# Transposing attention probabilities on VectorE and through DRAM instead of on TensorE, in a one-core hybrid block

## The chip, the cores and the metric

One core of a Trainium2 chip runs the whole kernel. The metric is the device time of one execution in microseconds, taken as the median of repeated runs. TensorE (PE) multiplies matrices, VectorE (DVE) and ScalarE (ACT) work element by element, GpSimd (POOL) does some adds here and issues DMAs of its own, and SyncE (SP) issues the other DMAs. A queue of an engine is worked off in the order of the program: what stands behind a waiting instruction waits too.

## The reference

A decoder block on 256 tokens of width 2048, in fp32. What matters for the change is the attention; the rest is one stream of weight matmuls.

```
proj = rmsnorm(x) @ w_in                     # pooled branch, queries, keys, values, gate inputs
y_a  = (pool_mixer(u) * silu(g_pool)) @ w_pool_out
# per kv head (4), per query head of it (4): compressed, selected and window branch
p_c  = softmax(mask(q @ kc.T * scale))       # 15 compressed keys
p_s  = softmax(mask(qh @ ks.T * scale))      # selected keys (256 tokens: all 4 blocks)
p_w  = softmax(mask(qh @ kw.T * scale))      # window keys
o    = g0 * (p_c @ vc) + g1 * (p_s @ vs) + g2 * (p_w @ vw)
y_b  = (o * silu(g_nsa)) @ w_nsa_out
gm   = sigmoid(h @ w_merge + b_merge)
out  = rmsnorm(x + (gm0 * y_a + gm1 * y_b) @ w_out)
```

The probabilities come out of the softmax with the query tokens on the partitions. The products with the values need the keys there, so every block of probabilities is transposed.

## The kernel before

**Numbers.** Each fp32 operand is split into a high and a low float32r part (`split`, L209 ff.: ACT copies the high part at L214, DVE subtracts it for the low part at L215), and each product is three matmuls (`mm3`, L226 to L229): high by high, high by low, low by high.

**Order.** The weights are streamed from DRAM in 314 units of up to 512 KB, in the order of `plan()`. For i = 0 to 3 come the chunks q(i), gn(i), m(i) and po(i) with 8, 8, 8 and 4 units; later m, no and wo. A unit is 12 matmuls of 128x512. The loop of `body` issues the load of a unit on SP six units ahead (`AHEAD`), its split three units ahead (`CUT`), then the unit's matmuls, and then `advance()`, which takes one piece of work from each of the lanes "e", "a", "c", "d", "b" in turn. The lanes hold generators; a `yield` ends a piece. So the program's order of small work between the units is set by how often a generator yields.

**Queries.** When chunk q(i) is done, `evac_q` applies the rotary embedding: two multiplications on DVE (L495, L498) and an add on GpSimd (L499), for each of two token blocks. `queries(i)` in lane "a" then calls `turn()`: DVE transposes 32x32 blocks (L275, a tile q1R for head 1), GpSimd writes it to DRAM (L281, q1W) and reads it back with four DMAs that put the blocks in their places (L285, qT). After `TURN` = 4 pieces the result is split into qh and ql (L214, L215), and the two attention pairs of head i are put into lane "b". `gate_t` does the same for the gate (gn).

**Attention.** `attend(hk, pr)` handles pair pr (0 or 1) of kv head hk, two query heads g each. Scores are three products of 272, 272 and 256 columns per g; each goes to a buffer of the PSUM tag "S", of which there are two, and DVE adds the mask and frees it (L710). The names S1000, S1001 and S1002 in this document are the scores of head 1, pair 0, g 0, product 0, 1 and 2. Then come the maxima (L716 to L721), the exponentials on ACT (L731), and `weigh` (L742 to L750), which scales by gate and sum and leaves three weighted copies of the compressed part in Cn. The transposes are matmuls with the identity: four per g in `turn1` (L756, second token block), two per g in `turn0` (L763), and two of Cn (L798), into PSUM tag "T". Each group is split from PSUM by ACT and DVE into P1h, P1l, P0 and Pc. `values` multiplies with the values (L818 and `mm3`) some steps later.

The tiles of tag "B" (46 blocks of 128x1056) hold weights, their parts, queries, scores and probabilities alike.

Of the kernel before, what the change touches and what calls it, by code (L numbers as in the profile page):

```python
# [11 lines left out]
F32 = mybir.dt.float32  # L12
F32R = mybir.dt.float32r
BF16 = mybir.dt.bfloat16
AF = mybir.ActivationFunctionType
OP = mybir.AluOpType
# [172 lines left out]
def body(nc, tc, d, out):  # L189
# [5 lines left out]
    dp = tc.alloc_tile_pool(name="dp", bufs=1, space=bass.MemoryType.DRAM)  # L195

    def blk(dt, name):
        return sb.tile([128, NB], dt, tag="B", bufs=NBLK, name=name)
# [7 lines left out]
    def psum(tag, name):  # L206
        return pp.tile([128, 512], F32, tag=tag, bufs={"P": 4, "S": 2, "T": 2}[tag], name=name)

    mm, act, dve, pool = nc.tensor.matmul, nc.scalar.activation, nc.vector, nc.gpsimd  # L209

    def split(hi, lo, src, scale=None, eng=None):

        if scale is None:
            act(hi, src, AF.Copy)  # L214
            (eng or dve).tensor_tensor(lo, src, hi.bitcast(F32), op=OP.subtract)  # L215
        else:
            act(hi, src, AF.Copy, scale=scale)
            dve.scalar_tensor_tensor(lo, src, scale, hi.bitcast(F32), op0=OP.mult, op1=OP.subtract)
# [16 lines left out]
    def C(name):  # L235
        a, b = CONST[name]
        return ct[:, a:b]
# [5 lines left out]
    ss2 = cp.tile([128, 2, 5], F32, name="ss2")  # L243


    lanes = {k: deque() for k in "eacdb"}

    def later(lane, gen):
        lanes[lane].append(gen)
# [437 lines left out]
    def attend(hk, pr):  # L687
        nm = f"{hk}{pr}"
        Cn = small(192, f"Cn{nm}", bufs=2)
        Cv = Cn.rearrange("p (i c g n) -> p i c g n", i=2, c=3, g=2)  # L690
        P1h, P1l, P0 = blk(F32R, f"P1h{nm}"), blk(F32R, f"P1l{nm}"), blk(F32R, f"P0{nm}")
        v1h, v1l = (x[:, :1024].rearrange("p (k g q) -> p k g q", k=4, g=2) for x in (P1h, P1l))
        v0h, v0l = (P0[:, a:a + 512].rearrange("p (k g q) -> p k g q", k=2, g=2) for a in (0, 512))
        qh, ql = qTt[hk]
        Ss, cfs = {}, {}

        SC = ((0, 0, 272, 0, C("m0")), (1, 0, 272, 272, C("m1")), (1, 272, 528, 544, C("m0")[:, 16:]))

        def scores(g, js):
            hd = pr * 2 + g  # L700
            if g not in Ss:
                Ss[g] = blk(F32, f"S{nm}{g}")
            Sg = Ss[g]
            for j in js:
                tok, a, b, o, m = SC[j]
                ps = psum("S", f"S{nm}{g}{j}")[:, :b - a]
                qo = hd * 256 + tok * 128
                kh, kl = kth(hk, a, b)
                mm3(ps, qh[:, qo:qo + 128], ql[:, qo:qo + 128], kh, kl, True, True)
                dve.tensor_tensor(Sg[:, o:o + b - a], ps, m, op=OP.add)  # L710

        def probs(g):
            Sg = Ss[g]
            mx = small(6, f"mx{nm}{g}")
            sm = small(6, f"sm{nm}{g}")
            dve.tensor_reduce(mx[:, 1:3], Sg[:, 16:272].rearrange("p (b k) -> p b k", b=2), axis=AX.X, op=OP.max)  # L716
            t1 = Sg[:, 288:800].rearrange("p (k b c) -> p b k c", k=2, b=2)
            dve.tensor_reduce(mx[:, 4:6], t1, axis=AX.XY, op=OP.max)
            cc = Sg[:, :544].rearrange("p (i c) -> p i c", i=2)[:, :, :16]
            dve.tensor_reduce(mx.rearrange("p (i b) -> p i b", i=2)[:, :, 0], cc, axis=AX.X, op=OP.max)  # L720
            dve.tensor_scalar(mx, mx, -1e29, -SCALE, op0=OP.max, op1=OP.mult)  # L721
            cfs[g] = mx, sm

        def expo(g):
            Sg = Ss[g]
            mx, sm = cfs[g]
            for i in range(2):
                for b in range(3):
                    k = i * 3 + b
                    s = part(Sg, i, b)  # L730
                    act(s, s, AF.Exp, bias=mx[:, k:k + 1], scale=SCALE, accum_out=sm[:, k:k + 1])  # L731

        def part(Sg, i, b):
            if b == 0:
                return Sg[:, i * 272:i * 272 + 16]
            if i == 0:
                return Sg[:, b * 128 - 112:b * 128 + 16]
            return Sg[:, 288:800].rearrange("p (k b c) -> p b k c", k=2, b=2)[:, b - 1]

        def weigh(g):  # L740
            Sg, sm = Ss[g], cfs[g][1]
            dve.tensor_tensor(sm[:, 0:1], sm[:, 0:1], C("inval"), op=OP.add)  # L742
            dve.reciprocal(sm, sm)
            dve.tensor_tensor(sm, sm, gates[:, hk * 4 + pr * 2 + g].rearrange("p i b -> p (i b)"), op=OP.mult)
            for i in range(2):
                dve.tensor_scalar(Cv[:, i, :, g], part(Sg, i, 0)[:, None, :].to_broadcast([128, 3, 16]),
                                  sm[:, i * 3:i * 3 + 1], None, op0=OP.mult)
                for b in range(1, 3):
                    s = part(Sg, i, b)
                    dve.tensor_scalar(s, s, sm[:, i * 3 + b:i * 3 + b + 1], None, op0=OP.mult)  # L750

        def turn1(g):
            Sg = Ss[g]
            p1 = psum("T", f"p1{nm}{g}")
            for k in range(4):
                nc.tensor.transpose(p1[:, k * 128:k * 128 + 128], Sg[:, 288 + k * 128:416 + k * 128], C("ident"))  # L756
            split(v1h[:, :, g], v1l[:, :, g], p1.rearrange("p (k q) -> p k q", k=4))

        def turn0(g):
            Sg = Ss[g]  # L760
            p0 = psum("T", f"p0{nm}{g}")
            for k in range(2):
                nc.tensor.transpose(p0[:, k * 128:k * 128 + 128], Sg[:, 16 + k * 128:144 + k * 128], C("ident"))  # L763
            split(v0h[:, :, g], v0l[:, :, g], p0[:, :256].rearrange("p (k q) -> p k q", k=2))

        if pr == 0:
            yield
            yield
        scores(0, (0, 1))
        yield  # L770
        scores(0, (2,))
        probs(0)
        yield
        expo(0)
        yield
        scores(1, (0, 1))
        yield
        scores(1, (2,))
        probs(1)
        yield  # L780
        weigh(0)
        expo(1)
        yield
        yield
        turn1(0)
        yield
        turn0(0)
        weigh(1)
        yield
        yield  # L790
        turn1(1)
        yield
        turn0(1)
        yield

        pc = psum("T", f"pc{nm}")
        for i in range(2):
            nc.tensor.transpose(pc[:96, i * 128:i * 128 + 128], Cn[:, i * 96:i * 96 + 96], C("ident"))  # L798
        Pc = half(F32R, f"Pc{nm}")
        Pv = Pc[:96].rearrange("p (i g q) -> p i g q", i=2, g=2)  # L800
        pcv = pc[:96, :256].rearrange("p (i q) -> p i q", i=2)
        for g in range(2):
            act(Pv[:, :, g], pcv, AF.Copy, scale=C("pair")[:96, g:g + 1])
            dve.scalar_tensor_tensor(Pv[64:96, :, g], pcv[64:96], C("pair")[64:96, g:g + 1],
                                     Pv[64:96, :, g].bitcast(F32), op0=OP.mult, op1=OP.subtract)
        later("d", values(hk, pr, Pv, v0h, v0l, v1h, v1l))

    def values(hk, pr, Pv, v0h, v0l, v1h, v1l):
        nm = f"{hk}{pr}"
        yield  # L810
        yield
        po = psum("T", f"po{nm}")
        pov = po.rearrange("p (g t) -> p g t", g=2)
        hs = slice(hk * 128, hk * 128 + 128)
        hs2 = slice(512 + hk * 128, 640 + hk * 128)
        for i in range(2):
            o = pov[:, :, i * 128:i * 128 + 128]
            mm(o, vstk[:, hk], Pv[:, i], start=True, stop=False)  # L818
            n = 2 * (i + 1)
            vh, vl = (v0h, v0l) if i == 0 else (v1h, v1l)  # L820
            for k in range(n):
                V = Vt[k // 2, k % 2]
                mm3(o, V[:, hs], V[:, hs2], vh[:, k], vl[:, k], False, k == n - 1)
        yield
        if pr == 0:
            yTt[hk] = (blk(F32R, f"yh{hk}"), blk(F32R, f"yl{hk}"))
        t = half(F32, f"y{nm}")
        cs = slice(pr * 512, pr * 512 + 512)
        dve.tensor_tensor(t.rearrange("p (g c j) -> p g c j", g=2, j=32), po.rearrange("p (g c j) -> p g c j", g=2, j=32),
                          by_head(gnT[hk])[:, pr * 2:pr * 2 + 2], op=OP.mult)  # L830
        yield
        split(yTt[hk][0][:, cs], yTt[hk][1][:, cs], t, eng=pool)
# [306 lines left out]
TURN = 4  # L1139
NTURN = 4  # L1140
# [43 lines left out]
```

## Time and profile before

| | us |
|---|---|
| median of 3 runs | 900.69 (899.91 to 901.51) |
| the profiled execution | 899.8 |
| its span | 898.0 |
| PE busy | 888.4 (99%) |
| DVE busy | 593.7 (66%) |
| ACT busy | 464.0 (52%) |
| POOL busy | 156.7 (17%) |
| mean granted TensorE clock | 0.997 |

The span is the time from the first to the last instruction on the core; 1.8 us of the execution lie outside it. Busy shares are means over stages of different kinds. A chain of waits follows the work that ended last back from the end: its pieces don't overlap, while the durations of neighbouring matmuls do. A timeline gives start and duration of each instruction, and in brackets how long the engine was idle before it and what ended that. The name in brackets is the releaser that the profile infers; for a read-back behind its own write it can name another engine that happened to finish then.

### The profile page before, as it was taken

The page shows a single profiled execution, that of the slowest core. Times are in us where ns is not written, and L with a number is a line of the kernel's source. Part 1 is how long each engine was busy: PE and PEld are TensorE (multiplying, and loading weights), DVE is VectorE, ACT ScalarE, POOL GpSimd, SP SyncE. Part 2 cuts the span into 40 slices and gives each one's busy share as a digit, 9 for nine tenths or more (in the row PEclk, how much of TensorE's full clock was granted, in tenths as well). Part 3 has the DMA queues.
Part 4 walks back from the last instruction along what each step waited for, and adds up shares of the span by engine and source line. Part 5 has one row for each costly group of instructions (what it writes and reads, how often), then busy time and mean ns, then how long its engine had stood idle before and what let it go on. Part 6 is the DMA issues. An engine that isn't in the chain of part 4 may idle for free.

```text
span 898.0 us, 11882 instructions
## 1 busy us (share of the span) xinstructions
PE 888.4 (99%) x4289; PEld 748.0 (83%) x4289; DVE 593.7 (66%) x889; ACT 464.0 (52%) x726; POOL 156.7 (17%) x145
## 2 busy tenths in 40 slices
PE   9999999999999999999999999999999999999996
PEld 7999988888888888888888888888888888888886
DVE  7756457877747476868685868687765565547633
ACT  7666545635734365456645664566554434436510
POOL 2203235333002110212021202110002312111110
PEclk9999999999999999999999999999999999999998
DMA  9955675778865664576557654766566776986602
GB/s 341 401 171 181 220 257 182 230 240 286 282 232 177 194 202 147 170 218 201 172 155 215 210 167 139 241 203 213 171 194 218 233 223 214 305 292 213 218 1 93
DMA packets 56298, 189.02 MB, mean 210 GB/s; under 512 B 6960, under 2 KB 7728, under 8 KB 56240
## 3 DMA queue, kind: packets, MB, share of 16 engines
q1 hardware_dynamic: 50912, 172.40, 59.0%
q0 software_dynamic: 5040, 15.73, 5.8%
q8 instruction: 33, 0.54, 0.2%
q14 instruction: 25, 0.20, 0.1%
q10 hardware_dynamic: 288, 0.14, 0.1%
HBM read 178.29 MB, written 9.96 MB: 210 GB/s over the span
## 4 chain that ended last, share of the span: by engine, by line
PE 98%; DMA 1%; DVE 0%; ACT 0%; SPq 0%; issue 0%; DVEq 0%; ACTq 0%
PE m L229 7%; PE m L228 7%; PE m L227 7%; PE p L228 3%; PE p L227 3%; PE p L229 3%; PE wo L229 3%; PE gn L229 3%; PE gn L228 3%; PE q L228 3%; PE q L229 3%; PE wo L227 3%; PE no L228 3%; PE wo L228 3%; PE gn L227 3%; PE no L227 3%
## 5 line engine op out<-in xcount | busy, mean ns | idle before, releaser
L215 DVE TENSOR_TENSOR l<-w,h 128x1024 fp32r<-128x1024 f32 (+2 forms) x312 | 388.1, 1270 | 76.7 <-ACT h L214 69.3
L214 ACT ACTIVATE h<-w 128x1024 fp32r<-128x1024 f32 (+2 forms) x312 | 308.5, 1031 | 66.4 <-PE no L228 13.4
L227 PE MATMUL m<-h,xh 128*128 128x512 f32 x256 | 101.3, 396 | 0.0
L229 PE MATMUL m<-h,xl 128*128 128x512 f32 x256 | 100.9, 394 | 0.0
L228 PE MATMUL m<-l,xh 128*128 128x512 f32 x256 | 100.7, 393 | 0.0
L227 PE MATMUL p<-h,xh 128*128 128x420 f32 (+1 forms) x160 | 57.4, 359 | 0.4 <-ACT h L1090 0.3
L229 PEld LDWEIGHTS m<-h,xl 128*128 128x128 f32 x256 | 48.0, 188 | 11.2
L228 PE MATMUL p<-l,xh 128*128 128x420 f32 (+1 forms) x160 | 56.7, 354 | 0.2 <-DVE l L1096 0.2
L229 PE MATMUL p<-h,xl 128*128 128x420 f32 (+1 forms) x160 | 56.5, 353 | 0.0
L227 PEld LDWEIGHTS m<-h,xh 128*128 128x128 f32 x256 | 48.2, 188 | 9.9
L228 PEld LDWEIGHTS m<-l,xh 128*128 128x128 f32 x256 | 48.2, 188 | 10.0
L731 ACT ACTIVATE S<-S,mx 128x16 f32<-128x16 f32 (+2 forms) x96 | 37.7, 394 | 34.9 <-DVE mx L721 34.8
L227 PE MATMUL wo<-h,mh 128*128 128x512 f32 (+1 forms) x144 | 53.2, 369 | 0.0
L229 PE MATMUL wo<-h,ml 128*128 128x512 f32 (+1 forms) x144 | 53.1, 368 | 0.0
L228 PE MATMUL wo<-l,mh 128*128 128x512 f32 (+1 forms) x144 | 52.9, 367 | 0.0
L227 PE MATMUL gn<-h,xh 128*128 128x512 f32 x128 | 51.6, 403 | 0.0
L227 PE MATMUL q<-h,xh 128*128 128x512 f32 x128 | 51.0, 398 | 0.0
L229 PE MATMUL gn<-h,xl 128*128 128x512 f32 x128 | 50.4, 394 | 0.0
L229 PE MATMUL q<-h,xl 128*128 128x512 f32 x128 | 50.4, 394 | 0.0
L228 PE MATMUL gn<-l,xh 128*128 128x512 f32 x128 | 50.4, 394 | 0.0
L228 PE MATMUL q<-l,xh 128*128 128x512 f32 x128 | 50.4, 394 | 0.0
L228 PE MATMUL no<-l,yh 128*128 128x512 f32 x128 | 50.3, 393 | 0.0
(339 smaller groups left out, 1771.8 us busy)
## 6 DMA issues: line engine op xcount, KB each, us to landing
w<-wts SPq DMA_DIRECT2D x274, 512.0 KB, 4.2
w<-wts SPq DMA_DIRECT2D x30, 420.0 KB, 7.6
w<-wts SPq DMA_DIRECT2D x8, 416.0 KB, 3.7
bb<-bmr SPq DMA_DIRECT2D x8, 256.0 KB, 4.4
xr<-xn SPq DMA_DIRECT2D x4, 512.0 KB, 4.8
out<-ot SPq DMA_DIRECT2D x8, 256.0 KB, 2.5
xs<-xT SPq DMA_DIRECT2D x7, 256.0 KB, 7.3
bt<-bic SPq DMA_DIRECT2D x2, 512.0 KB, 8.5
```

The lines of the kernel that those rows point to most:

```text
L214: act(hi, src, AF.Copy)
L215: (eng or dve).tensor_tensor(lo, src, hi.bitcast(F32), op=OP.subtract)
L227: mm(o, ah, bh, start=start, stop=False)
L228: mm(o, ah, bl, start=False, stop=False)
L229: mm(o, al, bh, start=False, stop=stop)
L731: act(s, s, AF.Exp, bias=mx[:, k:k + 1], scale=SCALE, accum_out=sm[:, k:k + 1])
```

## The change

The 112 transposes on TensorE go. `turn_p(g)` puts in their place three block transposes on DVE per g (128x256 each; for g = 1 a fourth, of Cn, 128x192) into a tile R, one write to DRAM by GpSimd (tile Wp), and four reads back by GpSimd into a tile G (for g = 1 seven). `cut_p`, in a new lane "w" that stands ahead of "b", waits six pieces and then splits the parts of G into P1h, P1l and P0, one per piece, and Pc with the last. `attend` yields less: the second `weigh` comes one piece earlier, and the generator ends four pieces earlier, so that the next pair starts earlier. The layout of Pc and the view of the product with the compressed values follow.

```diff
-    lanes = {k: deque() for k in "eacdb"}
+    lanes = {k: deque() for k in "eacdwb"}
...
-        def turn1(g):
+        G = {}
+
+        def turn_p(g):
+
             Sg = Ss[g]
-            p1 = psum("T", f"p1{nm}{g}")
-            for k in range(4):
-                nc.tensor.transpose(p1[:, k * 128:k * 128 + 128], Sg[:, 288 + k * 128:416 + k * 128], C("ident"))
-            split(v1h[:, :, g], v1l[:, :, g], p1.rearrange("p (k q) -> p k q", k=4))
-
-        def turn0(g):
-            Sg = Ss[g]
-            p0 = psum("T", f"p0{nm}{g}")
-            for k in range(2):
-                nc.tensor.transpose(p0[:, k * 128:k * 128 + 128], Sg[:, 16 + k * 128:144 + k * 128], C("ident"))
-            split(v0h[:, :, g], v0l[:, :, g], p0[:, :256].rearrange("p (k q) -> p k q", k=2))
+            r = blk(F32, f"R{nm}{g}")
+            rv = r[:, :768].rearrange("p (b k j) -> p k b j", b=4, j=32)
+            for k, o in ((0, 16), (2, 288), (4, 544)):
+                dve.transpose(rv[:, k:k + 2], Sg[:, o:o + 256].rearrange("p (k b j) -> p k b j", k=2, b=4))
+            n = 768
+            if g:
+
+                dve.transpose(r[:, 768:960].rearrange("p (c i j) -> p i c j", c=3, j=32),
+                              Cn.rearrange("p (i c j) -> p i c j", i=2, j=32))
+                n = 960
+            w = dp.tile([128, 960], F32, tag="Wp", bufs=NTURN, name=f"Wp{nm}{g}")
+            pool.dma_start(w[:, :n], r[:, :n])
+            t = G[g] = blk(F32, f"G{nm}{g}")
+            for b in range(4):
+                pool.dma_start(t[32 * b:32 * b + 32, :768].rearrange("p (a x) -> p a x", a=4),
+                               w[:, b * 192:b * 192 + 192].rearrange("(a i) x -> i a x", a=4))
+            if g:
+                for c in range(3):
+                    pool.dma_start(t[32 * c:32 * c + 32, 768:1024].rearrange("p (a x) -> p a x", a=4),
+                                   w[:, 768 + c * 64:832 + c * 64].rearrange("(a i) x -> i a x", a=4))
...
         weigh(0)
         expo(1)
         yield
-        yield
-        turn1(0)
-        yield
-        turn0(0)
+        turn_p(0)
+        yield
         weigh(1)
         yield
-        yield
-        turn1(1)
-        yield
-        turn0(1)
-        yield
-
-        pc = psum("T", f"pc{nm}")
-        for i in range(2):
-            nc.tensor.transpose(pc[:96, i * 128:i * 128 + 128], Cn[:, i * 96:i * 96 + 96], C("ident"))
+        turn_p(1)
+        later("w", cut_p(hk, pr, G))
+
+    def cut_p(hk, pr, G):
+
+        nm = f"{hk}{pr}"
+        for _ in range(TURN + 2):
+            yield
+        P1h, P1l, P0 = blk(F32R, f"P1h{nm}"), blk(F32R, f"P1l{nm}"), blk(F32R, f"P0{nm}")
...
+        for g in range(2):
+            t = G[g][:, :768].rearrange("p (a k j) -> p k a j", a=4, j=32)
+            q4 = [x[:, :, g].rearrange("p k (a j) -> p k a j", j=32) for x in (v1h, v1l, v0h, v0l)]
+            split(q4[0], q4[1], t[:, 2:])
+            yield
+            split(q4[2], q4[3], t[:, :2])
+            if g == 0:
+                yield
         Pc = half(F32R, f"Pc{nm}")
-        Pv = Pc[:96].rearrange("p (i g q) -> p i g q", i=2, g=2)
-        pcv = pc[:96, :256].rearrange("p (i q) -> p i q", i=2)
+        Pv = Pc[:96].rearrange("p (g a i j) -> p i g a j", g=2, a=4, i=2)
+        pcv = G[1][:96, 768:1024]
```

In the rows of order below, a name's number tells buffers of one name apart; w, h and l are a weight unit and its two parts, yph and ypl the parts of the pooled branch.

TensorE at the first removed group, between the last unit of chunk m(0) and the first of po(0). Before:

```order
L227 MATMUL m_2850<-h_2965,xh_287 128x512
L228 MATMUL m_2850<-l_2966,xh_287 128x512
L229 MATMUL m_2850<-h_2965,xl_288 128x512
L756 MATMUL p_3063<-ct,S_2860 128x128 x4
L227 MATMUL po_3076<-h_2994,yph_1271 128x512
L228 MATMUL po_3076<-l_2995,yph_1271 128x512
```

Now:

```order
L227 MATMUL m_2847<-h_2962,xh_287 128x512
L228 MATMUL m_2847<-l_2963,xh_287 128x512
L229 MATMUL m_2847<-h_2962,xl_288 128x512
L227 MATMUL po_3086<-h_2991,yph_1271 128x512
L228 MATMUL po_3086<-l_2992,yph_1271 128x512
```

The four transposes of the scores' tile S are gone, and the units follow one another.

GpSimd ahead of the queries of head 2 (yl are low parts of the gated output). Before:

```order
L285 DMA gnT_3719<-gn1W 32x8x128 x4
L215 TENSOR_TENSOR yl_3330<-y_3722,yh_3329 128x512
L215 TENSOR_TENSOR yl_4162<-y_4163,yh_4161 128x512
L499 TENSOR_TENSOR q2r0a<-q2r0a,q2r0b 128x512
L499 TENSOR_TENSOR q2r1a<-q2r1a,q2r1b 128x512
L281 DMA q2W<-q2R 128x1024
L285 DMA qT_4317<-q2W 32x8x128 x4
```

Now:

```order
L765 DMA Wp_4170<-R_4166 128x768
L768 DMA G_4172<-Wp_4170 32x4x192 x4
L765 DMA Wp_4231<-R_4226 128x960
L768 DMA G_4233<-Wp_4231 32x4x192 x4
L772 DMA G_4233<-Wp_4231 32x4x64 x3
L499 TENSOR_TENSOR q2r0a<-q2r0a,q2r0b 128x512
L499 TENSOR_TENSOR q2r1a<-q2r1a,q2r1b 128x512
L281 DMA q2W<-q2R 128x1024
L285 DMA qT_4336<-q2W 32x8x128 x4
```

The two writes and eleven reads of head 1's second pair stand right ahead of the adds for head 2's queries, and the gated output's parts have moved behind them.

DVE from the split of head 2's queries to its first score adds. Before:

```order
L215 TENSOR_TENSOR ql_4316<-qT_4317,qh_4315 128x1024
L215 TENSOR_TENSOR l_4462<-w_4384,h_4461 128x1024
L215 TENSOR_TENSOR l_4484<-w_4409,h_4483 128x1024
L710 TENSOR_TENSOR S_4522<-S_4523,ct 128x272
L710 TENSOR_TENSOR S_4522<-S_4528,ct 128x272
```

Now:

```order
L215 TENSOR_TENSOR ql_4335<-qT_4336,qh_4334 128x1024
L215 TENSOR_TENSOR P_4449<-G_4172,P_4449 128x2x128
L215 TENSOR_TENSOR l_4478<-w_4409,h_4477 128x1024
L215 TENSOR_TENSOR P1l_4448<-G_4233,P1h_4447 128x4x128
L215 TENSOR_TENSOR l_4502<-w_4429,h_4501 128x1024
L215 TENSOR_TENSOR P_4449<-G_4233,P_4449 128x2x128
L822 SCALAR_TENSOR_TENSOR Pc_4521<-G_4233,ct,Pc_4521 32x256 x2
L707 TENSOR_TENSOR S_4526<-S_4527,ct 128x272
L707 TENSOR_TENSOR S_4526<-S_4532,ct 128x272
```

The splits of the pair before now stand between the queries' split and the score adds.

## Rows read from the trace of the kernel before

**Rows 1.** Waits of TensorE, grouped: total us, count, us of the longest.
```profile
PE warm L345 <- DVE zero L341: 1.2, 1, 1.2
```

**Rows 2.** Chain of waits, 325 to 350 us: start us, us, engine and line.
```profile
330.86 0.44 PE p L756 x4
...
334.08 0.22 PE p L763 x2
...
346.05 0.22 PE pc L798 x2
```

**Rows 3.** Instructions by line, TensorE: count | busy us, mean ns | idle before.
```profile
L756 PE MATMUL p<-ct,S 128*128 128x128 f32 x64 | 9.6, 272 | 0.0
...
L763 PE MATMUL p<-ct,S 128*128 128x128 f32 x32 | 6.1, 271 | 0.0
...
L798 PE MATMUL pc<-ct,Cn 128*96 128x128 f32 x16 | 3.0, 272 | 0.0
```

**Rows 4.** Timeline of TensorE, 364 to 403 us: start us, us, instruction.
```profile
364.23 0.28 PE L227 MATMUL S<-KT,qh 128*128 128x256 f32 x1
...
364.58 0.40 PE L227 MATMUL q<-h,xh 128*128 128x512 f32 x1
...
370.14 0.40 PE L227 MATMUL gn<-h,xh 128*128 128x512 f32 x1
...
402.56 0.28 PE L227 MATMUL S<-KT,qh 128*128 128x256 f32 x1
```

**Rows 5.** Timeline of DVE, 364 to 402 us.
```profile
369.88 1.22 DVE L215 TENSOR_TENSOR l<-w,h 128x1024 fp32r<-128x1024 f32 x1 [0.49 <-ACT h L214]
...
381.06 0.70 DVE L275 STREAM_TRANSPOSE q1R<-q1r1a 128x512 f32<-128x512 f32 x1
...
400.92 0.79 DVE L710 TENSOR_TENSOR S<-S,ct 128x272 f32<-128x272 f32 x2
```

**Rows 6.** Windows: us, busy PE, PEld, DVE, ACT, POOL, granted clock, DMA.
```profile
360.00:390.00 30.00, 30.00 (x143) 24.58 (x142) 24.57 (x49) 13.84 (x29) 8.78 (x8) 1.00 0.59 187
```

**Rows 7.** Instructions by line, ACT: busy us, mean ns | idle before, releaser.
```profile
L214 ACT ACTIVATE P1h<-p 128x512 fp32r<-128x512 f32 x16 | 9.6, 599 | 36.6 <-PE p L756 36.6
...
L803 ACT ACTIVATE Pc<-pc,ct 96x256 fp32r<-96x256 f32 x16 | 7.5, 471 | 18.3 <-PE pc L798 13.5 <-DVE Pc L804 4.7
```

**Rows 8.** Timelines of POOL, then ACT, the queries of head 1.
```profile
372.52 2.14 POOL L499 TENSOR_TENSOR q1r0a<-q1r0a,q1r0b 128x512 f32<-128x512 f32 x1 [8.16 <-DVE q1r0b L498]
374.85 1.30 POOL L499 TENSOR_TENSOR q1r1a<-q1r1a,q1r1b 128x512 f32<-128x512 f32 x1 [0.20 <-DVE q1r1b L498]
...
382.07 0.59 POOL L281 DMA_DIRECT2D q1W<-q1R  x1 [5.92 <-DMA w<-wts]
387.26 2.42 POOL L285 DMA_DIRECT2D qT<-q1W  x4 [4.60 <-ACT h L214]
...
394.09 1.06 ACT L214 ACTIVATE qh<-qT 128x1024 fp32r<-128x1024 f32 x1 [3.10 <-DMA qT<-q1W]
```

**Rows 9.** The same of heads 0 and 3.
```profile
291.62 0.59 POOL L281 DMA_DIRECT2D q0W<-q0R  x1 [2.02 <-DVE q0R L275]
295.54 2.43 POOL L285 DMA_DIRECT2D qT<-q0W  x4 [3.33 <-PE gn L229]
...
305.98 1.06 ACT L214 ACTIVATE qh<-qT 128x1024 fp32r<-128x1024 f32 x1 [15.33 <-DMA qT<-q0W]
...
562.60 0.59 POOL L281 DMA_DIRECT2D q3W<-q3R  x1 [5.92 <-DVE q3R L275]
569.18 2.41 POOL L285 DMA_DIRECT2D qT<-q3W  x4 [6.00 <-PE pc L798]
...
574.58 1.06 ACT L214 ACTIVATE qh<-qT 128x1024 fp32r<-128x1024 f32 x1 [2.76 <-DMA qT<-q3W]
```

**Rows 10.** Windows at the end, columns as in rows 6.
```profile
890.00:891.00 1.00, 0.11 (x1) 0.00 (x0) 0.82 (x2) 0.34 (x2) 0.00 (x0) 1.00 0.00 0
...
893.00:894.00 1.00, 0.00 (x0) 0.00 (x0) 1.00 (x3) 0.00 (x0) 0.00 (x0) 0.67 0.25 94
```

More of the change, by code (lines that the diff above doesn't have):

```diff
@@ L690, in attend @@
         Cv = Cn.rearrange("p (i c g n) -> p i c g n", i=2, c=3, g=2)
-        P1h, P1l, P0 = blk(F32R, f"P1h{nm}"), blk(F32R, f"P1l{nm}"), blk(F32R, f"P0{nm}")
-        v1h, v1l = (x[:, :1024].rearrange("p (k g q) -> p k g q", k=4, g=2) for x in (P1h, P1l))
-        v0h, v0l = (P0[:, a:a + 512].rearrange("p (k g q) -> p k g q", k=2, g=2) for a in (0, 512))
         qh, ql = qTt[hk]
@@ L783, in attend @@
         yield
+        turn_p(0)
         yield
-        turn1(0)
-        yield
-        turn0(0)
         weigh(1)
         yield
-        yield
-        turn1(1)
-        yield
-        turn0(1)
-        yield
-        pc = psum("T", f"pc{nm}")
-        for i in range(2):
-            nc.tensor.transpose(pc[:96, i * 128:i * 128 + 128], Cn[:, i * 96:i * 96 + 96], C("ident"))
+        turn_p(1)
[5 more added lines that the diff above has]
+        P1h, P1l, P0 = blk(F32R, f"P1h{nm}"), blk(F32R, f"P1l{nm}"), blk(F32R, f"P0{nm}")
+        v1h, v1l = (x[:, :1024].rearrange("p (k g q) -> p k g q", k=4, g=2) for x in (P1h, P1l))
+        v0h, v0l = (P0[:, a:a + 512].rearrange("p (k g q) -> p k g q", k=2, g=2) for a in (0, 512))
+        for g in range(2):
[6 more added lines that the diff above has]
+                yield
         Pc = half(F32R, f"Pc{nm}")
-        Pv = Pc[:96].rearrange("p (i g q) -> p i g q", i=2, g=2)
-        pcv = pc[:96, :256].rearrange("p (i q) -> p i q", i=2)
+        Pv = Pc[:96].rearrange("p (g a i j) -> p i g a j", g=2, a=4, i=2)
+        pcv = G[1][:96, 768:1024]
         for g in range(2):
-            act(Pv[:, :, g], pcv, AF.Copy, scale=C("pair")[:96, g:g + 1])
-            dve.scalar_tensor_tensor(Pv[64:96, :, g], pcv[64:96], C("pair")[64:96, g:g + 1],
-                                     Pv[64:96, :, g].bitcast(F32), op0=OP.mult, op1=OP.subtract)
+            hi = Pc[:96, g * 256:g * 256 + 256]
+            act(hi, pcv, AF.Copy, scale=C("pair")[:96, g:g + 1])
+            dve.scalar_tensor_tensor(hi[64:96], pcv[64:96], C("pair")[64:96, g:g + 1],
+                                     hi[64:96].bitcast(F32), op0=OP.mult, op1=OP.subtract)
         later("d", values(hk, pr, Pv, v0h, v0l, v1h, v1l))
@@ L817, in values @@
             o = pov[:, :, i * 128:i * 128 + 128]
-            mm(o, vstk[:, hk], Pv[:, i], start=True, stop=False)
+            mm(o.rearrange("p g (a j) -> p g a j", j=32), vstk[:, hk], Pv[:, i], start=True, stop=False)
             n = 2 * (i + 1)
```

## The prediction, made before the changed kernel had run

> **What bounds the kernel now.** I read the waits of TensorE first, because a kernel whose span is one engine's work is moved only by that engine's work or by a new wait on it. TensorE waits three times, all at the very start, the longest for 1.2 us [rows 1]. From there to the last matmul it runs without a hole, so two questions decide the change: how much TensorE time the removed transposes really took, and whether anything that TensorE needs now comes later than it wants it. For the first I read the chain of waits, since a chain's pieces add up to the span and durations of overlapping matmuls don't [rows 2, 3]. For the second I followed, from TensorE's score matmuls, what DVE, GpSimd and ACT do up to the next head's scores [rows 4 to 8].
>
> **What is removed.** In the chain a group of four transposes takes 0.44 us and a group of two 0.22 us, the first two of a probability block and the two of Cn alike [rows 2]. There are 64/4 = 16 groups of four, 32/2 = 16 and 16/2 = 8 groups of two [rows 3]. 16 x 0.44 + 16 x 0.22 + 8 x 0.22 = 7.0 + 3.5 + 1.8 = 12.3 us, all on the path. The busy times of those lines, 9.6 + 6.1 + 3.0 = 18.7 us, are no gain: they count the drain of one matmul beside the next [rows 3].
>
> **What is added beside the path.** 56 block transposes go to DVE. A 128x512 one took 0.70 us [rows 5], so one of 128x256 is estimated at 0.35 and the whole at 56 x 0.35 = 20 us, spread over some 350 us. In the fullest stretch DVE has 24.6 of 30 us [rows 6]. One pair adds 7 x 0.35 = 2.5 us there: 27 of 30, which the three units of 2.78 us that a weight split has in hand hide. If that cover went, each microsecond beyond it would stop TensorE for as long. The splits of P stay as many (ACT 0.60 and 0.47 us each [rows 7]); they read SBUF now and wait for no transpose. The attended values of a pair come six steps later, and nothing but the gated output waits for them. The blocks that carry R and G make weight loads wait longer for a free slot; those loads are asked for six units, 16.7 us, ahead. I cost these at nothing.
>
> **What is added on GpSimd, and the wait that it makes.** GpSimd gets 16 writes and 88 reads, in order. A read waits for its write to land, and whatever stands behind it on GpSimd waits too. Behind the last pair of heads 0, 1 and 2 stand the two rope adds of the next head's queries, its write and its reads. TensorE then needs qh and ql for the next scores. I count from the start of the last score of a pair (364.23 in the trace [rows 4]), as in the order of the new program:
>
> - DVE's weight split behind the weighing ends at +6.9 (369.88 + 1.22 [rows 5]). A split of P (0.6) and three transposes (1.0) follow: +8.5. A write goes out 0.3 us behind its transpose (381.76 to 382.07 [rows 5, 8]): +8.8.
> - From a write's issue to its first read 5.2 us passed at q1 [rows 8]; the six such pairs of q and gn of heads 1 to 3 run from 4.7 to 6.6, mean 5.3. First read +14.1; four issues take 2.42 us [rows 8]: +16.5. Only now the second write goes out: +5.3 is +21.8, seven issues of 0.605 are 4.2: +26.0.
> - The rope adds of the next head, 2.14 and 1.30 us with 0.2 before each [rows 8]: +29.85. DVE's second query transpose stands behind a weight split and ends at +30.9; the query write leaves at +31.2. In the trace of before that write waited for nothing of the kind.
> - From that write to the split of qh 12.0 us passed at heads 1 and 3 [rows 8, 9]; the mean of heads 1, 2 and 3 is 12.45: +43.65.
> - From qh to the end of the second score's add 7.6 us passed for both adds (394.09 to 400.92 + 0.79), 7.3 to the end of the first [rows 5, 8]. Four splits of P and two of Pc now stand between, of which about 1.9 us lies on the way (two Pc of 0.47 and two halves of P [rows 7]): the first add, which frees a score buffer, ends at +52.8.
>
> TensorE wants that buffer for the third score. In the trace 38.33 us lie between the last score of a pair and that third score (364.23 to 402.56 [rows 4]). The new order has four more weight units between them (16 for 12) and lacks 1.5 us of transposes; a unit is 2.78 us (364.58 to 370.14 are two [rows 4]): 38.33 - 1.54 + 11.1 = 47.9. So TensorE **stands still for 52.8 - 47.9 = 4.9 us**, of it about 1.3 already before the first score, where ql comes late. Before, the same score had 1.2 us in hand (402.56 less 401.36). This happens at heads 1, 2 and 3: 3 x 4.9 = 14.7 us. Head 0 has no attention before it, and after head 3 no queries follow.
>
> **Sum.** Profiled execution 899.8 - 12.3 + 14.7 = 902.2; that execution lies 0.9 below the median of 900.69: **903.0**. Without any standstill it would be 888.4, and each microsecond of standstill per head costs 3: time = 888.4 + 3X.
>
> Bounds of X: a write's landing counts twice, from 3.9 us (291.62 to 295.54) to 6.6 (562.60 to 569.18) [rows 9], which gives -2.7 to +2.6; at the short end the second write waits for its transpose at +15.1 instead. From write to qh it runs from 12.0 to 14.4 (291.62 to 305.98 [rows 9]): -0.4 to +2.0. X lies between 1.8 and 9.5, the time between 893.7 and 916.9. I take 5.3 and 12.45 because the rows of heads 1 to 3 stand in the same place with the same load traffic, and head 0's do not.
>
> **Rivals.**
>
> *Faster: the landings are short.* The probability writes are 384 and 480 KB instead of the queries' 512, and the reads move larger pieces for the same bytes. If X stays under 3.5, the time is 888.4 to 898.9, at the short end of both rows 893.7; with X = 0, 888.4. For it: 3.9 us was seen once, at head 0. Against it: every later pair took 4.7 or more, and seven reads stand where q had four.
>
> *Slower: the landings are long.* Eleven reads in pieces of 768 and 256 bytes share the DMA engines with the weight loads, and the splits of P stand ahead of the score adds on both engines. From X = 6.2 on it is slower than 907; at 7.5 it is 910.9, at both long ends 916.9. For it: head 3's 6.6 us. Against it: two of three heads gave 12.0 from write to qh.
>
> *Slower: the pause lets the clock fall.* After the last matmul at 890.1 the granted clock was still 1.00 in that microsecond and 0.67 in the one from 893 [rows 10]; one of the standstills, 3.5 us in one piece at the third score, is as long. At half speed, 1.2 GHz, a unit takes 5.6 us; if the clock took as long to return as it took to fall, 3.5 us, a fall would cost 1.7 us, three of them 5: 903.0 + 5 = 908. I count it with the long landings. The Trainium skill, "TensorE: Matmul & The Clock Gate", section "Part 1: The HAM clock gate", says that an idle TensorE is put back to its lower clock; the end of this trace agrees, and by that rule each of the three standstills risks a fall.
>
> *Far slower: GpSimd can't issue beside DVE.* If each issue first waited for the end of a DVE operation, a weight split of 1.22 us [rows 5], the 18 issues from the first write to the last query read would be up to 22 us later at each head: 66 in all, 969. Against it: four issues in a stretch where DVE is busy for 24.6 of 30 us took 2.42 us, 0.605 each [rows 6, 8]. The Trainium skill, "SBUF — State Buffer", section "A bandwidth-pool intuition that's wrong", speaks for such a wait: GpSimd can't write descriptors while VectorE holds the shared port, and a DMA of about 620 ns took about 3100; by that, 18 x 2.5 us at three heads are 135 us, an estimated 1038. The issues of this trace don't show it, and the measurement decides.
>
> **How the numbers follow.** Forecast (X from 3.5 to 6.2, 898.9 to 907.0) 0.42; short landings 0.33; long landings or a fallen clock (907 to 917) 0.20; blocked issues 0.03; a cause that I don't see, slower, 0.02. About 0.2%, 1.8 us, is what a measurement of this kernel tells from no change. Of the forecast, X under 4.7 (902.5) is within it: 0.19; above, 0.23. Faster 0.33, same 0.19, slower 0.23 + 0.20 + 0.05 = 0.48. Below 891.5 I leave 0.09 (X under 1), above 913 0.11 (X over 8.2). The likeliest case alone has 898.9 to 907.
>
> **What would show it.** In the new trace: no transposes on TensorE, and its busy time lower by 12 us or more; three waits of TensorE, each at the start of head 1, 2 or 3, at the third score for DVE's add and at the first for ql; GpSimd idle before each first read for 4 to 6 us, and the query write about 31 us behind the last score of the pair; the granted clock at 1.00 through them. The prediction is wrong if TensorE waits elsewhere, at weight splits above all (DVE or ACT full), or if it doesn't wait at all (the landings are short, 888). The step on which it hangs is the write's landing, counted twice, then the 12.45 us of the queries.

## The result, and the profile of the changed kernel

The changed kernel takes 911.17 us (median of 4 runs, 907.52 to 912.36) against 901.1 us before: a ratio of 1.0106, with an interval of 1.0074 to 1.0137. It is slower by some 10 us. Predicted were 903.0 us and a range of 891.5 to 913.0. The sign was that of the forecast, and so were the places of three standstills and the chain of causes behind them. The size was that of a rival, the fallen clock, and of a fourth standstill that no case had.

The profiled execution has a span of 909.8 us, 11.8 more than before. First the page's line of busy times, then the waits of TensorE (total us, count, the longest), which answer to [rows 1]:

```profile
PE 884.1 (97%) x4177; PEld 742.0 (82%) x4177; DVE 607.4 (67%) x945; ACT 463.9 (51%) x726; POOL 208.3 (23%) x249
...
PE S L227 <- DVE S L707: 12.6, 4, 3.8
PE S L229 <- DVE ql L215: 1.5, 2, 0.7
PE warm L345 <- DVE zero L341: 1.2, 1, 1.2
PE S L227 <- ACT qh L214: 1.0, 1, 1.0
PE p L228 <- DVE l L215: 0.6, 1, 0.6
PE vs L228 <- DVE l L215: 0.6, 1, 0.6
```

The score's waits for its buffer, for qh and for ql are new and make 12.6 + 1.5 + 1.0 = 15.1 us; two waits of 0.6 for weight splits, before the attention, are 1.2, where the kernel before had 0.5 there. So TensorE stands still for about 16 us more. Its busy time has fallen by only 4.3 us, though 12.3 us of transposes are gone. Most of the difference of 8.0 us is the clock. These are the windows of one microsecond around the standstill at head 1 (columns as in rows 6):

```profile
399.00:400.00 1.00, 0.00 (x0) 0.00 (x0) 1.00 (x1) 1.00 (x4) 0.00 (x0) 1.00 0.30 123
400.00:401.00 1.00, 0.00 (x0) 0.00 (x0) 0.97 (x4) 1.00 (x2) 0.00 (x0) 1.00 0.00 0
401.00:402.00 1.00, 0.15 (x1) 0.15 (x1) 0.97 (x3) 0.81 (x1) 0.00 (x0) 0.71 0.00 0
402.00:403.00 1.00, 1.00 (x4) 0.99 (x5) 1.00 (x2) 0.00 (x0) 0.00 (x0) 0.50 0.55 143
403.00:404.00 1.00, 1.00 (x4) 0.72 (x3) 1.00 (x3) 0.00 (x0) 0.00 (x0) 0.50 0.79 315
404.00:405.00 1.00, 1.00 (x4) 0.81 (x3) 1.00 (x3) 0.00 (x0) 0.00 (x0) 0.58 0.16 66
405.00:406.00 1.00, 1.00 (x6) 0.79 (x6) 0.97 (x4) 0.50 (x1) 0.00 (x0) 1.00 0.00 0
```

TensorE is idle for 3.47 us here, the granted clock falls to 0.50 (1.2 GHz) shortly before it starts again at 401.85, and until 405 a matmul of 128x512 starts every 0.43 us instead of every 0.23. Busy share times the missing part of the clock, added up over such windows, is 1.5 us for this fall. Two falls at head 3 cost 1.7 each, and one in head 3's second pair 1.7: 6.6 us in all. At those three the clock fell when TensorE had been at work again for 0.8 to 1.3 us. Some 1.4 us more, an estimate, are hidden in the busy time: a wait is counted from the modelled end of the matmul before it, 0.39 us after that one's start, while in a dense stream the next one starts after 0.23, so that each of the nine waits is 0.16 us longer than its row says. The span is then 15.8 us of standstill, 6.6 of clock and 1.4 hidden, less 12.3 of transposes: 11.5 of the 11.8 us.

The chain that the forecast counted, at head 2. The zero is the last score of head 1's second pair. From POOL's timeline (the probabilities' writes and reads, then head 2's queries), then ACT, then DVE, then TensorE; in brackets the idle time and what ended it:

```profile
457.99 0.56 POOL L765 DMA_DIRECT2D Wp<-R  x1 [0.70 <-DVE R L761]
466.25 2.19 POOL L768 DMA_DIRECT2D G<-Wp  x4 [7.70 <-DMA Wp<-R]
468.43 1.63 POOL L772 DMA_DIRECT2D G<-Wp  x3
470.08 1.29 POOL L499 TENSOR_TENSOR q2r0a<-q2r0a,q2r0b 128x512 f32<-128x512 f32 x1
471.32 1.29 POOL L499 TENSOR_TENSOR q2r1a<-q2r1a,q2r1b 128x512 f32<-128x512 f32 x1
474.89 0.58 POOL L281 DMA_DIRECT2D q2W<-q2R  x1 [2.28 <-DVE y L847]
...
485.80 1.06 ACT L214 ACTIVATE qh<-qT 128x1024 fp32r<-128x1024 f32 x1 [6.81 <-DMA qT<-q2W]
...
464.21 0.75 DVE L498 TENSOR_TENSOR q2r1b<-q,sinr 128x256 f32<-128x256 f32 x2
...
471.41 0.71 DVE L275 STREAM_TRANSPOSE q2R<-q2r0a 128x512 f32<-128x512 f32 x1 [5.32 <-POOL q2r0a L499]
494.69 0.79 DVE L707 TENSOR_TENSOR S<-S,ct 128x272 f32<-128x272 f32 x2
...
442.25 0.28 PE L227 MATMUL S<-KT,qh 128*128 128x256 f32 x1
488.18 0.40 PE L229 MATMUL S<-KT,ql 128*128 128x272 f32 x1 [0.74 <-DVE ql L215]
495.18 0.38 PE L227 MATMUL S<-KT,qh 128*128 128x256 f32 x1 [3.45 <-DVE S L707]
```

GpSimd waits 7.7 us for the second write to land. The inputs of the rope adds are ready at 465, and the adds run at 470, right behind the last read. DVE's first query transpose waits 5.3 us for them at the head of DVE's queue. In [rows 8] the query write stood behind none of that.

The fourth standstill is at the third score of head 3's second pair (TensorE, DVE and POOL):

```profile
632.74 0.39 PE L227 MATMUL S<-KT,qh 128*128 128x256 f32 x1 [3.77 <-DVE S L707]
...
628.78 1.23 DVE L215 TENSOR_TENSOR l<-w,h 128x1024 fp32r<-128x1024 f32 x1 [5.53 <-DMA Wp<-R]
...
618.55 0.56 POOL L765 DMA_DIRECT2D Wp<-R  x1
629.52 2.18 POOL L768 DMA_DIRECT2D G<-Wp  x4 [10.41 <-DMA w<-wts]
```

Here no query waits. A weight unit's low part l waits on DVE until a write of R has landed: it is put into R's block, and the block is not free before the DMA has read it. The landing took 10 us, and the score adds stand behind that l. That it is R's block is inferred from the wait: R and l have the same tag B, and l has no other business with that write.

### The profile page after: what moved, and what is told of

Read it like the earlier page. It is cut to its first block, busy times and chain, and to the rows that moved or that the text cites. A ratio compares the mean times of both kernels' runs of the same rounds, so it can differ in the third digit from the quotient of the medians.

```text
span 909.8 us, 11953 instructions
## 1 busy us (share of the span) xinstructions
PE 884.1 (97%) x4177; PEld 742.0 (82%) x4177; DVE 607.4 (67%) x945; ACT 463.9 (51%) x726; POOL 208.3 (23%) x249
## 5 line engine op out<-in xcount | busy, mean ns | idle before, releaser
L214 ACT ACTIVATE h<-w 128x1024 fp32r<-128x1024 f32 (+2 forms) x312 | 309.5, 1031 | 119.8 <-PE m L228 15.7
L227 PE MATMUL m<-h,xh 128*128 128x512 f32 x256 | 103.2, 403 | 0.0
L228 PE MATMUL m<-l,xh 128*128 128x512 f32 x256 | 103.2, 403 | 0.0
L229 PE MATMUL m<-h,xl 128*128 128x512 f32 x256 | 103.0, 402 | 0.0
L228 PEld LDWEIGHTS m<-l,xh 128*128 128x128 f32 x256 | 49.7, 194 | 10.9
L768 POOL DMA_DIRECT2D G<-Wp x64 | 34.9, 552 | 85.4 <-DMA Wp<-R 32.9
L229 PE MATMUL no<-h,yl 128*128 128x512 f32 x128 | 50.3, 393 | 0.0
```

The lines of the kernel that those rows point to most:

```text
L227: mm(o, ah, bh, start=start, stop=False)
L228: mm(o, ah, bl, start=False, stop=False)
L229: mm(o, al, bh, start=False, stop=stop)
L768: pool.dma_start(t[32 * b:32 * b + 32, :768].rearrange("p (a x) -> p a x", a=4), w[:, b * 192:b * 192 + 192].rearrange("(a i) x -> i a x", ...
```

## The experiments

Two theories stood against each other for the standstills at the heads. The **queue theory** is the forecast's: reads that wait at the head of GpSimd's queue make the query adds late. The **split theory**: the splits of P between qh and the score adds on ACT and DVE are what is late. Beside them stood two questions of size: what a fall of the clock costs, and what the transposes had cost.

**Reads of G three pieces later.** The reads go into a lane of their own (`LATE = 3`), and the writes stay where they are:

```diff
+            later("r", read_p(g, w))
+
+        def read_p(g, w):
+            for _ in range(LATE):
+                yield
             t = G[g] = blk(F32, f"G{nm}{g}")
```

> The changed kernel, but GpSimd's reads of G are issued three pieces later, so that the next head's rope adds and query write stand ahead of the last pair's reads and no read waits long at the head of GpSimd's queue. Queue theory (the query adds are late because reads wait at the head of GpSimd's queue): the query write leaves about 7 us earlier, TensorE's waits at the starts of heads 1, 2 and 3 (11.3 us of the 15.1 new ones) go and the clock falls with them (5.0 of 6.6 us), the wait in head 3's second pair (3.8) stays: 911.2 - 16.3 = 895. Split theory (the score adds are late because the splits of P stand ahead of them on ACT and DVE): only the waits for qh and ql (2.5 us) go, the third score still waits 2 to 3.5 us per head: 905 to 909.

Measured: 895.56 us, a ratio of 0.9923 (0.9895 to 0.9951) to the kernel before. GpSimd's timeline at the same place, and TensorE's waits:

```profile
455.83 0.56 POOL L765 DMA_DIRECT2D Wp<-R  x1 [5.72 <-DVE R L761]
456.48 2.20 POOL L773 DMA_DIRECT2D G<-Wp  x4
460.55 2.14 POOL L499 TENSOR_TENSOR q2r0a<-q2r0a,q2r0b 128x512 f32<-128x512 f32 x1 [1.87 <-DVE q2r0b L498]
462.87 2.21 POOL L499 TENSOR_TENSOR q2r1a<-q2r1a,q2r1b 128x512 f32<-128x512 f32 x1 [0.18 <-DVE q2r1b L498]
467.36 0.58 POOL L281 DMA_DIRECT2D q2W<-q2R  x1 [2.27 <-DVE y L852]
...
PE S L227 <- DVE S L707: 5.6, 5, 2.0
PE warm L345 <- DVE zero L341: 1.2, 1, 1.2
PE p L227 <- ACT h L1113: 0.9, 1, 0.9
```

The adds now wait for DVE alone, as in [rows 8]; the query write leaves 7.5 us earlier (2.3 of it because the last score of the pair is that much earlier, at 439.96). The waits for qh and ql are gone, and the granted clock stays at 1.00 throughout the attention; this execution has one fall of 1.7 us at its very start, at 8 to 12 us. The queue theory said 895, the split theory 905 to 909: the queue is by far the larger cause. What remains, 5.6 us at third scores, is what the split theory describes. The fourth standstill went too, which the expectation had not: the write ahead of it landed after 6.0 us instead of 10.1. The edit also takes G's blocks three pieces later, so this run doesn't tell the queue from the blocks for that fourth one.

**Splits of P four pieces later** (heads 0 to 2; head 3 keeps its place):

```diff
-        for _ in range(TURN + 2):
+        for _ in range(TURN + (6 if hk < 3 else 2)):
```

> The changed kernel, but the splits of P for heads 0 to 2 come four pieces later (the product with the values with them), so that they stand behind the next head's first score adds on ACT and DVE; GpSimd's order is that of the changed kernel. Queue theory: qh comes as late as before (about 106 and 121 us after the same points), so the waits for qh and ql stay (2.5 us in all); the third score's waits shrink by the 1.9 us of splits each, from 3.5, 3.5 and 1.9 to 1.6, 1.6 and 0, and the clock falls of heads 1 and 3 go if a wait of 1.6 us doesn't bring one: 911.2 - 5.7 - 3 to 5 = 900 to 903. Split theory: the third score's waits go entirely (8.8 us) and the falls with them: 897 or less.

Measured: 918.3 us (ratio 1.0178, 1.0152 to 1.0205), slower than the changed kernel, which neither theory had. TensorE's waits:

```profile
PE S L227 <- DVE S L707: 14.8, 8, 5.9
PE gn L228 <- DVE l L215: 3.3, 2, 2.9
PE S L227 <- ACT qh L214: 1.7, 1, 1.7
```

The queue stayed as it was: the write at head 2 took 10 us to its first read, and DVE's query transpose stood still for 9.0 us (476.02, released by the rope add), with a weight split behind it, hence the 2.9 us. The splits were not removed from in front of score adds but moved in front of others: the eight waits lie at third scores of first and second pairs alike, and ahead of head 2's second pair (a wait of 2.5 us) the parts of P are now split right before the score adds. So the run doesn't measure what it was made for.

**Both edits.**

> Both edits together: reads of G three pieces later and splits of P four pieces later. Queue theory: hardly better than the late reads alone, 894 to 895. Split theory: clearly better than either alone, by 3 us or more. Either theory leaves the wait in head 3's second pair (3.8 us and 1.7 of clock), since head 3's splits are not moved; without it, 889 to 890.

Measured: 909.38 us (1.0084, 1.0058 to 1.0109). That is clearly worse than the late reads alone, by 14 us, and neither theory had it. The waits for score adds are 13.6 us instead of 5.6, 4.75 of them at head 3's second pair. Four pieces later is the wrong direction for the splits.

**Matmuls into the pauses:**

```diff
+            fill(hk, pr, g, js)
             for j in js:
...
+    def fill(hk, pr, g, js):
+        at = (hk, pr, g, js)
+        n = 6 if hk and at[1:] == (0, 0, (0, 1)) else 12 if hk and at[1:] == (0, 0, (2,)) or at == (3, 1, 0, (2,)) else 0
+        if n:
+            f = psum("T", "fill")
+            for _ in range(n):
+                mm(f, xh[0][:, :128], xh[0][:, 512:1024], start=True, stop=True)
```

> The changed kernel with matmuls that nobody reads put on TensorE right ahead of the waits: 6 of 128x512 (1.4 us) ahead of the first score and 12 (2.8 us) ahead of the third score of heads 1, 2 and 3, and 12 ahead of the third score of head 3's second pair. They lie inside the pauses, so the score comes no later. Clock theory (a pause of 3.5 us lets the granted clock fall, and that cost 6.6 us): the granted clock stays at 1.00 and the time is about 904.6. Rival (the pause costs only its own length): about 911, or more where a filler reaches beyond a pause.

Measured: 906.95 us (904.92 to 911.18; a ratio of 1.0065, 1.0043 to 1.0087), 4.2 less than the changed kernel. The fillers ahead of head 1's third score, and the window after them:

```profile
398.54 2.90 PE L693 MATMUL fill<-xh 128*128 128x512 f32 x12
...
402.00:403.00 1.00, 1.00 (x6) 0.81 (x5) 1.00 (x2) 0.00 (x0) 0.00 (x0) 1.00 0.71 266
```

No window of the attention has a granted clock under 1.00, so idle time of TensorE is what makes it fall. TensorE does 66 matmuls more, and the median is lower all the same. The size is not settled: the two intervals overlap, the 66 fillers are 15.2 us and the waits fell by 9.5, so that fillers reached beyond the pauses, and 4.2 is less than the 6.6 that the windows give.

**Each transpose twice:**

```diff
-            for k in range(4):
+            for k in (0, 1, 2, 3, 0, 1, 2, 3):
                 nc.tensor.transpose(p1[:, k * 128:k * 128 + 128], Sg[:, 288 + k * 128:416 + k * 128], C("ident"))
```

and in the same way the groups of two.

> The kernel before with each of its 112 transposes issued twice into the same place. It prices the removed work: the new groups stand on TensorE's path as the old ones do. Chain price (0.44 and 0.22 us a group): + 12.3 us, 913 to 914. Price from the changed kernel's units (a unit that lost a group of four starts its successor 0.35 us earlier, one that lost two 0.22): + 10.9 us, 912. Price by busy durations: + 18.7, 920.

Measured: 911.41 us against 900.69, +10.7 (ratio 1.0118; its interval is +8.6 to +12.6). In its chain of waits the doubled groups take twice the time that the single ones have in [rows 2]:

```profile
330.87 0.87 PE p L756 x8
...
334.52 0.44 PE p L763 x4
```

The chain's price, 12.3, and the 10.9 both lie in the interval; the durations' 18.7 does not.

**Reads two pieces later and splits two pieces earlier.** The edit of the late reads with `LATE = 2`, and

```diff
-        for _ in range(TURN + 2):
+        for _ in range(TURN + 0):
```

> The changed kernel with the reads of G two pieces later and the splits of P two pieces earlier, so that the splits stand ahead of the query split on ACT and DVE instead of between it and the score adds. Theory (what is left in the late-reads kernel, 5.6 us at third scores, is the 1.9 us of splits between qh and the score adds): those waits go, 895.6 - 5.6 = 890, which is the time before less the transposes. Rival (the splits now wait for the landings of G at the head of ACT's and DVE's queues, and weight splits behind them come late): TensorE waits for l or h instead, 895 or more.

Measured: 888.91 us (0.9865, 0.9837 to 0.9892), and in a second measurement:

> The kernel with the reads two pieces later and the splits two pieces earlier, once more with more rounds: 888 to 890, a ratio of 0.986 to 0.989 to the kernel before. 900.7 less the 10.7 to 10.9 us of transposes would be 889.9.

888.36 us against 901.1 (0.9861, 0.9845 to 0.9876). TensorE's waits in this second measurement, all of them:

```profile
PE S L227 <- DVE S L707: 1.3, 2, 0.8
PE warm L345 <- DVE zero L341: 1.2, 1, 1.2
PE p L228 <- DVE l L215: 0.6, 1, 0.6
PE p L228 <- DVE l L1119: 0.2, 1, 0.2
```

This is the prediction's 888.4 "without any standstill": the change is worth what its transposes cost, once next to nothing waits for its round trip. It beats both kernels.

**Splits three pieces earlier.** The same with one piece less:

> As the run before, but the splits of P three pieces earlier. Theory: 890 as well, or a little less where blocks come free earlier. Rival: G is read only two pieces ahead of its first split, so the splits wait for it, and TensorE's waits for weight splits grow: 895 to 905.

Measured: 903.8 us (1.0034, 1.002 to 1.0048): the rival's time. ACT's waits show its cause:

```profile
ACT P1h L214 <- DMA G<-Wp: 30.4, 9, 7.7
```

The splits stand at the head of ACT's queue until G has landed, weight splits and qh behind them; with the splits two pieces earlier this wait was 3.7 and 5.4 us in the two profiled executions. TensorE's waits are not where the rival put them: 0.5 us is for weight splits, 9.8 are at scores (5.8 for the buffer, 2.3 for qh, 1.7 for ql), and two falls of the clock cost 3.4. One piece, 2.8 us, decides between 889 and 904.

**Splits two pieces earlier alone**, with the changed kernel's GpSimd order:

> The changed kernel with the splits of P two pieces earlier, so that they stand ahead of the query split, and GpSimd's order as in the changed kernel: the second half of the 888.9 us kernel alone. Queue theory: the query write still stands behind G's last reads, so qh is hardly earlier and TensorE still waits at heads 1, 2 and 3, by 1.9 us less at each third score; with blocks free two pieces earlier head 3's second pair may lose its wait too: 897 to 904. Split theory (the splits between qh and the score adds are all of it): 889 to 892.

Measured: 908.45 us (1.0079, 1.0053 to 1.0105), above what either theory said and not clear of the changed kernel. The write at head 2 still leaves only at 474.41, and TensorE waits 6.6 us for qh:

```profile
474.41 0.58 POOL L281 DMA_DIRECT2D q2W<-q2R  x1 [2.28 <-DVE P1l L215]
...
PE S L227 <- ACT qh L214: 6.6, 2, 4.0
PE S L227 <- DVE S L707: 3.8, 3, 2.5
```

The waits for score adds fell from 12.6 to 3.8 us: there the splits had been the last to end, but the lateness came from the queue and shows one score earlier once they are away. The clock took 7.9 us here. With the late reads the four corners are: 911.2 as changed, 895.6 with the reads alone (three pieces), 908.5 with the splits alone, 888.4 with both (two pieces each).

**45 and 47 blocks.**

> The changed kernel with 45 blocks of tag B instead of 46. Block theory (the blocks that R and G hold make weight loads wait for a slot and then come in bunches; a write that falls into a bunch lands after 8 to 11 us instead of 3 to 5; and the low part of a weight unit waits for R's block until that write has landed, which made the fourth wait): one block less makes bunches and late writes more, 915 to 925. Rival (the long landings have nothing to do with blocks): 911 within 2.

Measured: 918.11 us (1.0196, 1.0169 to 1.0222).

> The changed kernel with 47 blocks of tag B, paid with 6 half tiles instead of 8. Block theory (45 blocks cost 7 us): one more block takes away waits on late writes, head 3's second pair loses its 3.8 us and the 1.7 us of clock, 903 to 907. Rival (46 are enough, and only fewer cost): 910 to 912. If the half tiles run short, slower than that.

Measured: 908.29 us (1.0075, 1.005 to 1.01), with no wait in head 3's second pair; the waits at heads 1, 2 and 3 stayed. One block less costs 7 us. One more gains 2.9 in the median, between what theory and rival said, and its interval overlaps that of the changed kernel; that the fourth standstill is a matter of blocks rests on the line of DVE above and on its absence here. The part of the block theory on landings isn't borne out. With 45 blocks the second writes ahead of heads 1, 2 and 3 took 9.4, 6.5 and 7.7 us to their first read, with 46 they took 6.3, 8.3 and 8.1. Nor do waits for a block that a write still reads grow in sum: ACT's and DVE's weight splits waited 9.9 us for such writes with 45 blocks, 15.3 with 46 and 13.7 with 47. What counts is where such a wait falls. This line of ACT with 45 blocks stands ahead of a standstill of 5.4 us in head 3's second pair:

```profile
634.42 1.06 ACT L214 ACTIVATE h<-w 128x1024 fp32r<-128x1024 f32 x1 [7.13 <-DMA Wp<-R]
```

How the rest of the 7 us comes about isn't shown.

## Why the prediction was right, and where its size was off

**The gain**, 12.3 us: right. The doubled transposes allow 8.6 to 12.6 us, and in the kernel of 888.4 us, with hardly a standstill, TensorE is busy for 875.8 us, 12.6 less than before.

**The chain at head 2**, from the last score of the pair (442.25), forecast and measured:

| step | forecast | measured |
|---|---|---|
| first write leaves | +8.8 | +9.5 |
| its first read | +14.1 | +12.7 |
| second write leaves | +16.5 | +15.7 |
| its first read | +21.8 | +24.0 |
| rope adds done | +29.85 | +30.4 |
| query write leaves | +31.2 | +32.6 |
| split of qh | +43.65 | +43.55 |
| first score add done, TensorE goes on | +52.8 | +52.9 |
| TensorE would have wanted it | +47.9 | +48.7 |
| standstill | 4.9 | 4.2 |

The measured times of the two rows above the last are 495.18, and 495.18 less the two waits of 3.45 and 0.74 us. The ends agree, but in part by luck: errors in the middle cancel. The two landings were set at 5.3 us each and were 3.2 and 8.3 (heads 1 and 3: 5.5 and 6.3, 5.5 and 8.1): at all three heads the second write, 480 KB, took longer than the first, 384 KB. From the query write to qh it was 10.9 to 11.1 us at all three heads instead of 12.45. The two rope adds took 1.29 us each instead of 2.14 and 1.30.

**The three standstills**: forecast 4.9 each, 14.7 in all; measured 3.47, 4.19 and 3.62, 11.3. The step is right and its term was too large by 3.4, of which the later point at which TensorE wants the score makes 0.8 at head 2.

**What was mis-sized is what follows a standstill.** The forecast of 903.0 gave the clock no term and kept it for a rival, with 1.7 us a fall and three falls. There were four, 1.5 to 1.7 us each and 6.6 in all: the price was right, but the sum left it out. Three falls were at the forecast standstills, though not one per head: head 2 had a pause of 3.45 us and no fall, head 1 one of 3.47 and a fall, and head 3 two falls after shorter pauses, 0.97 and 0.74 us and then 1.91. So the length of one pause doesn't tell whether the clock falls. The Trainium skill, "TensorE: Matmul & The Clock Gate", section "Part 1: The HAM clock gate", lets an idle TensorE drop to the lower clock; the windows above and the fillers agree.

**What was missing is the blocks.** "The blocks that carry R and G make weight loads wait longer ... I cost these at nothing" failed. It is not the loads that stopped TensorE but a split of weights, which gets R's block while the write still reads from it: 3.8 us and a fall, 5.5 in all, at a place that has no queries. The trace of before has two short waits of a split for a write, 1.4 us for q3's and 1.0 for m0's, and no long one, but with 46 blocks in use the question who gets R's block next could have been asked of the new program.

**The sum, term by term.** The forecast for the profiled execution was 902.2 us. Less 3.4 for the standstills, and with 3.8 for the fourth, 6.6 for the clock, 0.7 for weight splits before the attention and the estimated 1.4 that the waits hide, it is 911.3; measured were 911.6. So the result is in the range, but not in the forecast's own case of 898.9 to 907.0, and three of the signs that the prediction named went against it: TensorE's busy time fell by 4.3 us and not by 12, the granted clock did not stay at 1.00, and TensorE waited at a place that the forecast did not have.

**The rivals.** Faster needed X under 3.5; the mean was 3.8, so it was near, and the clock and the fourth standstill took it out of reach. GpSimd's issues took 0.55 us each beside DVE (64 of them 34.9 us), so the blocked issues didn't come. DVE's cover held: apart from the two waits of 0.6 us before the attention, TensorE waited for no weight split.

## What to carry to other kernels

On GpSimd's queue here, a DMA that reads back what an earlier one wrote blocked everything behind it until that write had landed, up to 7.7 us ahead of the queries of head 2; issue the write early and the read some pieces later, behind the work of others that is urgent, and put what consumes it no nearer than its landing. Work taken off the bounding engine pays back its full price only when that engine then waits for no round trip; with two numbers, how late the reads and how early the splits, this change went from 1.1% slower to 1.4% faster. In the changed kernel 15.1 us of TensorE's standstills cost 6.6 more through its clock, so a few short pauses were dearer than their sum.

## What the runs showed of the hardware

A GpSimd add of two 128x512 tiles took 1.29 to 1.31 us when it began while DVE rested or read PSUM, and 2.14 to 2.21 us when it began beside a weight split of DVE, which reads two SBUF tiles; an add delays DVE in turn. In the kernel before, q1's first add (372.52, 2.14 us) began beside the first split below. Its second add ran from 374.85 to 376.15, and the second split, which began beside it, took 1.95 us instead of 1.2:

```profile
372.29 1.21 DVE L215 TENSOR_TENSOR l<-w,h 128x1024 fp32r<-128x1024 f32 x1
...
375.28 1.95 DVE L215 TENSOR_TENSOR l<-w,h 128x1024 fp32r<-128x1024 f32 x1
```

The Trainium skill, "SBUF — State Buffer", section "Who interferes with whom", says that a VectorE instruction with two SBUF inputs contends with a GpSimd instruction that reads SBUF, and that the later one waits; these rows agree.

Writes to DRAM of nearly the same size landed after very different times. The page of the changed kernel's profile lists the medians from issue to landing (KB each, us):

```profile
Wp<-R POOLq DMA_DIRECT2D x8, 480.0 KB, 6.4
...
Wp<-R POOLq DMA_DIRECT2D x8, 384.0 KB, 3.1
```

A quarter more bytes took twice the time in the median, and one write took 10.1 us (issued at 618.55, the l that waited for it ran at 628.78) where seven weight loads were issued within 13 us. Why the two differ was not tried on its own, and that the loads are the cause is not shown.
